# The gated merge, output projection and retrieval scores of a decoder layer in two halves of the tokens, and 160 gathered tokens in place of 128

## The chip, the core and the metric

The kernel runs on one core of one Trainium2 chip. The core has five engines with a program each: TensorE (PE) multiplies matrices, VectorE (DVE) and ScalarE (ACT) work element by element, GpSimd (POOL) here issues gathers, SyncE (SP) issues transfers. They meet through semaphores. Data comes from HBM by 16 DMA engines into SBUF, which has 128 partitions; PE writes to PSUM. The metric is the device time of one launch in microseconds, lower is better; the median of several runs counts.

## The reference

One layer of a decoder for 512 tokens of 2048 float32 features: two token mixers side by side (a gated linear recurrence, HGRN2, and a latent attention, MLA), a gated merge and an output projection, then the PEER mixer, a gated embedding and a last norm. What the change touches:

```python
y = sigmoid(ga) * (o_a @ w_a) + sigmoid(gb) * (o_b @ w_b)    # ga, gb: two products of the normed input
x = x + y @ w_o
x = x + peer_ffn(rms_norm(x, norm_ffn), peer_wq, peer_k1, peer_k2, peer_u, peer_v)
hp = rms_norm(x, norm_ple)
x = x + sigmoid(hp @ w_pg) * (p @ w_pe)
...
def peer_ffn(h, wq, k1, k2, u_tab, v_tab):      # 8 heads, 128 keys in each half, 16384 experts
    q = (h @ wq).reshape(N, HEADS, 2, 128)
    s1, s2 = q[:, :, 0] @ k1.T, q[:, :, 1] @ k2.T
    v1, i1 = top_k(s1, 16); v2, i2 = top_k(s2, 16)
    cand = (v1[..., :, None] + v2[..., None, :]).reshape(N, HEADS, 256)
    cv, ci = top_k(cand, 16)
    e = i1[ci // 16] * 128 + i2[ci % 16]         # 8 heads * 16 = 128 experts for a token
    gate = softmax(cv)
    z = einsum('thkd,td->thk', u_tab[e], h)
    return einsum('thk,thkd->td', gelu(z) * gate, v_tab[e])
```

## The kernel before

**Products.** Each float32 product is done as three float32r matmuls of a high and a low part (`mm3`, L147 to L149: high by high, low of the data by high of the weights, high of the data by low of the weights). Weights come in blocks of 128x2048 (1 MB), each in two halves: SP loads a half into one of four `raw` buffers, ACT makes the high part (`hi`, L111), DVE the low part (`lo`, L112), in rings of four. `Ahead` loads a block two steps before it is used and splits it one step before. A block holds 16 tiles of 128x128, so 48 matmuls, whose width is the number of tokens that pass through (512, or 384 in PEER's dense part).

**Stages.** The recurrence runs to about 460 us, then attention. The gates are 32 weight blocks put between the attention heads and beside the loading of the merge's inputs (`FILL`, `fill_in`). Then come merge (`w_a`, `w_b`), output projection (`w_o`, with the sum of squares for the next norm), the embedding (`w_pe`, 96 matmuls), each for all 512 tokens, and the normed input h of PEER in 16 chunks (`h_chunk`, L682). Up to here a scheduler orders the instructions by their dependencies; from the query product on the order is written by hand (`manual_schedule`).

**PEER.** The 512 tokens are treated in two ways. The first 128 (group A, `NA`) gather the rows of their experts: POOL issues an indirect DMA for one of 128 slots (a row of 2048 for each of 128 tokens, 1 MB), DVE multiplies it by h and sums (`dot_u`, L785), and in the second half adds it to the output with its coefficient (`axpy_v`, L1083). The other 384 (group B, `NB`) go through all 16384 experts densely: 128 blocks of U (L1028), whose result z goes through gelu to HBM (`z_s`); a matrix of gates is built from one-hot rows (`gate_tokens`, L833, L843) and stored (`G_s`); 128 blocks of V multiply the product of the two (L1003, split by L154 and L155, added up by L1091). The top-k of the scores, by repeated MAX, index and replace (L692 to L697), runs on DVE in steps with costs written by hand, spread over the query product (group A) and over U (three groups of 128 tokens in group B). In V one row is added per block, in 120 of 128 blocks. Two row buffers serve the gathers.

**Queues.** SP issues weight loads and the loads of z and gates; ACT issues the stores of z and of scores, and an issue that waits holds what is behind it on ACT; POOL issues the gathers.

Of the kernel before, what the change touches and what calls it, by code (L numbers as in the profile page):

```python
# [22 lines left out]
KT = 16  # L23
NA = 128
NB = T - NA
# [21 lines left out]
def kernel(ctx: ExitStack, tc: tile.TileContext, a, dbg=None):  # L47
# [14 lines left out]
    # ---------------------------------------------------------------- helpers  # L62
# [14 lines left out]
    class Ring:  # L77
        """Buffers taken in turn."""
# [42 lines left out]
    class Ahead:  # L121
        """Streams of a list of blocks: loaded two steps ahead, split one step ahead."""
# [28 lines left out]
    def split(hi, lo, src, gain=None):  # L151
        """hi + lo = src * gain, both float32r."""
# [7 lines left out]
    def cols_proj(src, xh, xl, kt=KT):  # L160
        """PSUM [128 output columns, T] for one column tile."""
# [6 lines left out]
    def rows_proj(srcs, blocks, before=None):  # L168
        """PSUM [128 tokens, 512 columns] for each token block."""
# [12 lines left out]
    def rstd_cols(ss, n, name):  # L182
        """[128 tokens, blocks] of 1/sqrt(ss/n + eps)."""
# [13 lines left out]
    def sums_over_features(sq):  # L197
        """[128 tokens, 4] PSUM sums over the partitions of sq [128, T]."""
        ps = mx()
        for b in range(4):  # L200
            TE.matmul(ps[:, b:b + 1], lhsT=sq[:, b * 128:(b + 1) * 128], rhs=ones[:, :1],
                      start=True, stop=True)
        return ps[:, :4]
# [14 lines left out]
    class SumSq:  # L218
        """Sum of squares of [128, T] chunks over features."""

        def __init__(self, acc=None):
            self.acc = tmp.tile([128, T], F32, name="sqacc", bufs=1) if acc is None else acc
            self.n = 0

        def add(self, x):
            if self.n == 0:
                S.activation(self.acc, x, AF.Square)
            else:
                s = t2()
# [8 lines left out]
    # ---------------------------------------------------------------- constants  # L238
    masks = const.tile([128, 384], F32R, name="masks")
# [3 lines left out]
    tril = const.tile([128, 128], U32, name="tril")  # L243
# [16 lines left out]
    # ---------------------------------------------------------------- DRAM scratch  # L260
    ga_s = [dram.tile([128, T], F32, name=f"ga{i}") for i in range(16)]
    gb_s = [dram.tile([128, T], F32, name=f"gb{i}") for i in range(16)]
# [4 lines left out]
    pe_s = [dram.tile([128, T], F32, name=f"pe{i}") for i in range(16)]  # L267
    z_s = dram.tile([128 // NJ, 128, NJ, NB], F32, name="z_s")
    G_s = dram.tile([NB // TC, 128, 128 * TC], F32, name="G_s")

    # ---------------------------------------------------------------- x * gain, split
# [11 lines left out]
    hg = tc.alloc_tile_pool(name="hg", bufs=1, side="left")  # L283

# [15 lines left out]
    # ---------------------------------------------------------------- HGRN2  # L300
# [172 lines left out]
    # rotary tables: angle = position * frequency, reduced to [-pi, pi]  # L473
# [36 lines left out]
    gates_todo = [(a["w_ga"][i], ga_s[i]) for i in range(16)] + [(a["w_gb"][i], gb_s[i]) for i in range(16)]  # L510
    FILL = (0, 2)
# [864 lines left out]
```

## Time and profile before

| what | value |
|---|---|
| runs | 4041.33, 4042.06, 4043.58 us, median 4042.06 |
| profiled execution, span from first to last instruction | 4040.0 us |
| PE busy | 4005.3 us (99%) |
| DVE, ACT, POOL busy | 2621.1, 1597.2, 347.6 us |
| mean granted PE clock | 0.998 |
| moved by DMA | 862.68 MB, 214 GB/s in the mean |

The page gives one execution, whose span of 4040.0 us is the profiled time itself; the runs were timed apart from it and lie 1.3 to 3.6 us above. PE is busy almost throughout, and a busy engine is the first candidate for what sets the time; whether the others merely keep up is read stage by stage, from the busy time in windows and from who waits for whom.

### The profile page before, as it was taken

The numbers are of one execution on the slowest core, as the hardware profiler recorded it, in microseconds if no ns is written. First come the engines' busy times: TensorE is split into PE (matmuls) and PEld (weight loads), VectorE is DVE, ScalarE is ACT, GpSimd is POOL, SyncE is SP. The second block draws the span as 40 slices with busy tenths as digits, with TensorE's granted clock in tenths as the row PEclk, the third lists the DMA queues.
The fourth block names the chain that finished last, engine by engine and source line by source line (L and its number), as shares of the span: only waits on it lengthen the run. The fifth ranks groups of instructions, "written<-read, shape, count | busy, mean of one in ns | idle before, by whom it ended". The sixth has DMA issues, their size and how long they took to land. (4 is left out here: it accounts for less than half of the span.)

```text
span 4040.0 us, 54629 instructions
## 1 busy us (share of the span) xinstructions
PE 4005.3 (99%) x21191; PEld 3667.2 (91%) x21191; DVE 2621.1 (65%) x3992; ACT 1597.2 (40%) x2582; POOL 347.6 (9%) x262
## 2 busy tenths in 40 slices
PE   9999999999999999999999999999999999999998
PEld 7878777778888889999999999999999999999976
DVE  5352554443343343699998998977777888877744
ACT  5342433332332242325566555753333333333443
POOL 0000000000000000021221211111111111111000
PEclk9999999999999999999999999999999999999999
DMA  5222222334444442478787788789888888888432
GB/s 210 97 74 94 72 96 84 102 105 141 151 141 133 141 140 99 166 286 304 283 303 283 287 302 298 293 332 356 317 297 315 312 311 312 299 313 310 169 117 97
DMA packets 264515, 862.68 MB, mean 214 GB/s; under 512 B 24128, under 2 KB 94272, under 8 KB 229568
## 3 DMA queue, kind: packets, MB, share of 16 engines
q1 hardware_dynamic: 202064, 531.57, 38.5%
q0 software_dynamic: 36864, 268.45, 17.8%
q10 hardware_dynamic: 25328, 59.17, 3.8%
q8 instruction: 168, 2.75, 0.3%
q14 instruction: 91, 0.75, 0.1%
HBM read 780.44 MB, written 78.64 MB: 213 GB/s over the span
## 5 line engine op out<-in xcount | busy, mean ns | idle before, releaser
L111 ACT ACTIVATE hi<-raw 128x1024 fp32r<-128x1024 f32 x806 | 851.4, 1059 | 1606.9 <-PE acc L148 1371.9
L112 DVE TENSOR_TENSOR lo<-raw,hi 128x1024 fp32r<-128x1024 f32 x806 | 975.0, 1221 | 782.6 <-ACT hi L111 779.5
L147 PE MATMUL acc<-hBh,hi 128*128 128x384 f32 x2304 | 775.0, 336 | 0.0
L148 PE MATMUL acc<-hBl,hi 128*128 128x384 f32 x2304 | 774.5, 336 | 0.0
L149 PE MATMUL acc<-hBh,lo 128*128 128x384 f32 x2304 | 774.4, 336 | 0.0
L148 PEld LDWEIGHTS acc<-hBl,hi 128*128 128x128 f32 x2304 | 433.1, 188 | 3.0 <-DVE hBl L155 0.2
L147 PEld LDWEIGHTS acc<-hBh,hi 128*128 128x128 f32 x2304 | 433.1, 188 | 2.7
L149 PEld LDWEIGHTS acc<-hBh,lo 128*128 128x128 f32 x2304 | 433.1, 188 | 0.0
L779 POOL DMA_INDIRECT row<-in_peer_u_dram,eA x128 | 198.9, 1554 | 2551.1 <-DMA raw<-in_uT_dram 1703.2
L149 PE MATMUL acc<-xh,lo 128*128 128x512 f32 x912 | 363.9, 399 | 0.0
L147 PE MATMUL acc<-xh,hi 128*128 128x512 f32 x912 | 363.4, 398 | 0.0
L148 PE MATMUL acc<-xl,hi 128*128 128x512 f32 x912 | 362.6, 398 | 0.0
L147 PE MATMUL acc<-ahx,hi 128*128 128x384 f32 x1024 | 344.7, 337 | 0.0
L148 PE MATMUL acc<-alx,hi 128*128 128x384 f32 x1024 | 344.1, 336 | 0.0
L149 PE MATMUL acc<-ahx,lo 128*128 128x384 f32 x1024 | 344.1, 336 | 0.0
L147 PE MATMUL acc<-ah,hi 128*128 128x384 f32 x1024 | 344.1, 336 | 0.0
L148 PE MATMUL acc<-al,hi 128*128 128x384 f32 x1024 | 344.1, 336 | 0.0
L149 PE MATMUL acc<-ah,lo 128*128 128x384 f32 x1024 | 344.1, 336 | 0.0
L1083 DVE SCALAR_TENSOR_TENSOR outA<-row,coef,outA 128x2048 f32<-128x2048 f32 x127 | 298.0, 2346 | 16.6 <-DMA row<-in_peer_v_dram,eA 16.3
L785 DVE SCALAR_TENSOR_TENSOR row<-row,hrow 128x2048 f32<-128x2048 f32 x128 | 292.0, 2283 | 20.5 <-DMA row<-in_peer_u_dram,eA 20.4
L779 POOL DMA_INDIRECT row<-in_peer_v_dram,eA x128 | 147.5, 1152 | 860.3 <-DVE outA L1083 799.6
L149 PEld LDWEIGHTS acc<-xh,lo 128*128 128x128 f32 x912 | 171.4, 188 | 43.0 <-issue 2.4
(379 smaller groups left out, 6270.5 us busy)
## 6 DMA issues: line engine op xcount, KB each, us to landing
raw<-in_uT_dram SPq DMA_DIRECT2D x256, 512.0 KB, 6.9
raw<-in_vB_dram SPq DMA_DIRECT2D x256, 512.0 KB, 5.7
z_s<-t ACTq DMA_DIRECT2D x128, 192.0 KB, 4.9
G_s<-stage ACTq DMA_DIRECT2D x12, 2048.0 KB, 14.4
zt<-z_s SPq DMA_DIRECT2D x32, 768.0 KB, 7.4
gt<-G_s SPq DMA_DIRECT2D x32, 768.0 KB, 12.1
raw<-in_w_ga_dram SPq DMA_DIRECT2D x32, 512.0 KB, 3.5
raw<-in_w_gb_dram SPq DMA_DIRECT2D x32, 512.0 KB, 3.5
```

Of the source, the lines that this page charges most:

```text
L111: S.activation(hi, raw, AF.Copy)
L112: V.tensor_tensor(lo, raw, hi.bitcast(F32), op=OP.subtract)
L147: TE.matmul(out, lhsT=lh, rhs=rh, start=start, stop=False)
L148: TE.matmul(out, lhsT=lh, rhs=rl, start=False, stop=False)
L149: TE.matmul(out, lhsT=ll, rhs=rh, start=False, stop=stop)
L779: G.indirect_dma_start(out=row, out_offset=None, in_=tab, in_offset=bass.IndirectOffsetOnAxis(ap=eA[:, s:s + 1], axis=0))
L785: V.scalar_tensor_tensor(row, row, 1.0, hrow, op0=OP.mult, op1=OP.mult, accum_out=zA[:, s:s + 1])
L1083: V.scalar_tensor_tensor(outA, row, coef[:, s:s + 1], outA, op0=OP.mult, op1=OP.add)
```

## The change

Tokens 0 to 255 (the first half) now go through gates, merge, output projection, embedding, norm and scores before tokens 256 to 511 (the second half) do the same; each half multiplies 256 columns, so the weights of gates, `w_a`, `w_b`, `w_o`, `w_pe` and `wq` are loaded and split twice. The first half is left to the scheduler; the second is part of the order written by hand. While it runs, `background` does the top-k of token groups 0 and 1 and the first 26 dots of gathered rows. The gathered tokens grow from 128 to 160: the 32 new ones (`NX`) are spread over 128 partitions as 4 slots for each token, so their 128 experts take 32 gathers in U and 32 in V. The dense part has 352 columns (`ND`). Gathers have three row buffers. The query product makes columns for all tokens, where before group A's part was made by rows and transposed.

The diff, cut to its core (comments and docstrings are removed throughout, too, and line numbers move):

```diff
 NA = 128
-NB = T - NA
+NX = 32
+RX = 128 // NX
+ND = T - NA - NX
+NE = H - NA - NX
...
-        ps = cols_proj(src, xh, xl)
-        t = t2()
-        V.tensor_tensor(t, ps, rr_mix, op=OP.mult)
+        w = Stream(src)
+        ps = acc()[:, :H]
+        for k in range(KT):
+            mm3(ps, *w.part(k, KT), xh[:, k, :H], xl[:, k, :H], k == 0, k == KT - 1)
+        t = t2()[:, :H]
+        V.tensor_tensor(t, ps, rr_mix[:, :H], op=OP.mult)
...
+    def block(src):
+        if not manual[0]:
+            return Stream(src)
+        w = ahead.step()
+        run_late()
+        background()
+        return w
+
...
+    def embed_half(hf, ph, pl, sq, rr):
+
+        for i in range(2):
+            w = block(a["w_pe"][i])
+            for m in range(0, 8, 2):
+                ps = mx()
+                for c in range(2):
+                    for k in range(2):
+                        mm3(ps[:, c * H:c * H + H], *w.part((m + c) * 2 + k, 16), ph[:, k], pl[:, k], k == 0, k == 1)
+                t = t2()
+                S.activation(t, ps, AF.Copy)
+                nc.scalar.dma_start(flat(pe_s[hf][i * 4 + m // 2]), t)
+                if (i, m) == (0, 2):
+                    rc = rstd_cols(sums_over_features(sq.acc), D, "rc_ffn")
+                if (i, m) == (1, 2):
+                    rows_of(rc, rr)
+            done()
+
+    def h_chunk(k, x1, rr, hh, hl, kept=None):
+        t = t2()[:, :H]
+        V.scalar_tensor_tensor(t, x1[:, k], g_ffn[:, k:k + 1], rr, op0=OP.mult, op1=OP.mult)
+        split(hh, hl, t)
+        if kept is not None:
+            nc.scalar.dma_start(kept, t[:, NA + NX:])
+
...
+                S.activation(q, ps, AF.Copy)
+                return lambda: keys(i, q)
+
+            if manual[0]:
+                late.append(lambda query=query, turn=turn: turn.append(query()))
+            else:
+                query()()
+        return turn
+
...
-    def h_chunk(kt):
-        t = t2()
-        V.scalar_tensor_tensor(t, x1[:, kt], g_ffn[:, kt:kt + 1], rr, op0=OP.mult, op1=OP.mult)
-        split(hAh[:, kt], hAl[:, kt], t[:, :NA])
-        split(hBh[:, kt], hBl[:, kt], t[:, NA:])
...
+    embed_half(0, ph, pl, sq, rr)
+    for k in range(KT):
+        h_chunk(k, x1, rr, hAh[:, k], hAl[:, k], hd_s[:, k])
...
+    for k in range(KT):
+        r = t2()[:, :H]
+        nc.sync.dma_start(r, a["xT"][k][:, H:])
+        V.scalar_tensor_tensor(r, r, g_mix[:, k:k + 1], rr_mix[:, H:], op0=OP.mult, op1=OP.mult)
+        split(xBh[:, k], xBl[:, k], r)
...
-            t["scores"] = upool.tile([128, 16, 128], F32, name="scores")
-            if b:
-                nc.sync.dma_start(flat(t["scores"]), sc_s[b])
-            else:
-                scores_A.append(t["scores"])
+            t["scores"] = kpool.tile([128, 16, 128], F32, name="scores")
+            nc.scalar.dma_start(flat(t["scores"]), sc_s[b])
...
-    pending = None
-    for cg in range(4):
-        qA, qB = mx(), [acc()[:, :NB] for _ in range(4)]
-        for kq in range(4):
-            if cg == 0:
-                for k in range(4):
-                    h_chunk(kq * 4 + k)
-            w = ahead.step()
...
+    NEARLY = 26
+    todo = prep_A() + merge(prep_B(1), [(2.5, dot_u)] * NEARLY)
+    NB2 = 80
+    todo = phase(NB2, todo)
+    spent, at = [0.0], [0]
+
+    def background():
+        at[0] += 1
+        hold[0] = max(0, hold[0] - 1)
+        while todo and spent[0] < at[0] and not hold[0] and len(after_pe) < 2:
+            c, f = todo.pop(0)
+            f()
+            spent[0] += c
+
...
+    for n, (src, dst) in enumerate((("w_ga", ga_s[1]), ("w_gb", gb_s[1]))):
+        for i in range(16):
+            w = block(a[src][i])
+            ps = acc()[:, :H]
+            for k in range(KT):
+                mm3(ps, *w.part(k, KT), xBh[:, k], xBl[:, k], k == 0, k == KT - 1)
+
+            def gate(i=i, ps=ps, dst=dst):
+                t = t2()[:, :H]
+                S.activation(t, ps, AF.Sigmoid)
+                nc.scalar.dma_start(dst[i], t)
+
+            late.append(gate)
+            after_products()
+            if n:
+                mixed(i, 1, oh, ol)
+    run_late()
...
+    embed_half(1, ph, pl, sq, rr)
+    for k in range(KT):
+        h_chunk(k, x1, rr, hBh[:, k, NE:], hBl[:, k, NE:])
+    last_keys = scores_half(1, lambda k: hBh[:, k, NE:], lambda k: hBl[:, k, NE:])
...
+    upool = tc.alloc_tile_pool(name="upool", bufs=1, side="left")
+    NF, NW = 3, 116
+    MIX = (36, 46)
+    prep = prep_B(2)
+    work = phase(MIX[0], merge(prep[:-1], quads[1]) + prep[-1:])
+    prep = prep_B(3)
+    work += phase(MIX[1], merge(prep[:-1], quads[2]) + prep[-1:])
+    work += phase(NW - NF - sum(MIX), quads[3])
...
-        z = acc()[:, :NB]
+            spent += c
+        while dots[0] and LEFT + 1 - dots[0] <= LEFT * n / (NU - 2) + 1e-9:
+            dot_u()
+        z = acc()[:, :ND]
...
-            late = []
+            run_late()
             act_mul(grp + 1, dp)
-            while axpys and 129 - len(axpys) <= 128 * (n + 1) / NV + 1e-9:
-                axpy_v(axpys.pop(0))
+            while axpys and NDOT + 1 - axpys <= NDOT * (n + 1) / NV + 1e-9:
+                axpys -= 1
```

Three places in the order of the instructions, as the programs stand. The first is ACT's program at the seam between the halves: `t` are chunks of the second half's input, `xBh` their high parts, `scores<-sc_187` the issue of the load of group 0's scores, `hi_78` the high part of a gate block's weights.

```order
L158 ACTIVATE xBh<-t_10336 128x256
L859 DMA scores<-sc_187 128x2048
L158 ACTIVATE xBh<-t_10341 128x256
L158 ACTIVATE xBh<-t_10346 128x256
L158 ACTIVATE xBh<-t_10351 128x256
L158 ACTIVATE xBh<-t_10356 128x256
L158 ACTIVATE xBh<-t_10361 128x256
L158 ACTIVATE xBh<-t_10366 128x256
L158 ACTIVATE xBh<-t_10371 128x256
L158 ACTIVATE xBh<-t_10376 128x256
L158 ACTIVATE xBh<-t_10381 128x256
L115 ACTIVATE hi_78<-raw_74 128x1024
```

The stores of the last scores (`sc_187`, `sc_188`) stand directly ahead of these rows; before, neither chunks of the input nor a score load stood between the gates and the merge. The second is DVE at the same seam; `xBl` are the chunks' low parts, `val` the largest scores of group 0.

```order
L159 TENSOR_TENSOR xBl<-t_10361,xBh 128x256
L819 SCALAR_TENSOR_TENSOR t_10366<-t_10366,gains,rr_mix 128x256
L846 MAX val<-scores 128x8 x2
L848 MAX_INDEX idx<-val,scores 128x8
L159 TENSOR_TENSOR xBl<-t_10366,xBh 128x256
L819 SCALAR_TENSOR_TENSOR t_10371<-t_10371,gains,rr_mix 128x256
L819 SCALAR_TENSOR_TENSOR t_10376<-t_10376,gains,rr_mix 128x256
L819 SCALAR_TENSOR_TENSOR t_10381<-t_10381,gains,rr_mix 128x256
L159 TENSOR_TENSOR xBl<-t_10371,xBh 128x256
L159 TENSOR_TENSOR xBl<-t_10376,xBh 128x256
L159 TENSOR_TENSOR xBl<-t_10381,xBh 128x256
```

Behind these rows come the other chunks, then eight additions `t<-hAh,hAl` for h by rows, and then the low parts of the next blocks. Before, group A's MAX stood behind parts of the query product. The third is DVE at the norm ahead of the query product: first of before, where `lo` are low parts of weights.

```order
L682 SCALAR_TENSOR_TENSOR t_9288<-x_8051,gains,rr_ffn 128x512
L155 TENSOR_TENSOR hAl<-t_9288,hAh 128x128
L155 TENSOR_TENSOR hBl<-t_9288,hBh 128x384
L682 SCALAR_TENSOR_TENSOR t_9294<-x_8051,gains,rr_ffn 128x512
L155 TENSOR_TENSOR hAl<-t_9294,hAh 128x128
L155 TENSOR_TENSOR hBl<-t_9294,hBh 128x384
L112 TENSOR_TENSOR lo_80<-raw_72,hi_76 128x1024
L112 TENSOR_TENSOR lo_81<-raw_73,hi_77 128x1024
L682 SCALAR_TENSOR_TENSOR t_9366<-x_8051,gains,rr_ffn 128x512
```

Four chunks stood there for each weight block. In the changed kernel, second half, a lookup and a dot stand ahead and the chunks stand in one piece, 16 of them, before the next weights:

```order
L116 TENSOR_TENSOR lo_82<-raw_74,hi_78 128x1024
L116 TENSOR_TENSOR lo_83<-raw_75,hi_79 128x1024
L929 SCALAR_TENSOR_TENSOR row_7019,zA<-row_7019,hrow 128x2048
L215 TENSOR_SCALAR t_14999<-cst,rc_ffn 128x128 x2
L723 SCALAR_TENSOR_TENSOR t_15037<-x_B,gains,rrB 128x256
L159 TENSOR_TENSOR hBl<-t_15037,hBh 128x256
L723 SCALAR_TENSOR_TENSOR t_15041<-x_B,gains,rrB 128x256
L159 TENSOR_TENSOR hBl<-t_15041,hBh 128x256
L723 SCALAR_TENSOR_TENSOR t_15045<-x_B,gains,rrB 128x256
```

The place of V, where the rows are added, reads as follows in the changed kernel (`hrow` is now the sum of the gathered rows, `x` the dense one, `zt` and `gt` the z and the gates that come back):

```order
L1231 TENSOR_TENSOR x_26682<-x_26682,acc 128x352
L1150 TENSOR_TENSOR zt_26266<-zt_26266,gt_26268 128x352
L1222 SCALAR_TENSOR_TENSOR hrow<-row_7017,zA,hrow 128x2048
L1222 SCALAR_TENSOR_TENSOR hrow<-row_7018,zA,hrow 128x2048
L159 TENSOR_TENSOR alx_26696<-zt_26266,ahx_26688 128x352
L1231 TENSOR_TENSOR x_26682<-x_26682,acc 128x352
L116 TENSOR_TENSOR lo_82<-raw_74,hi_78 128x1024
L116 TENSOR_TENSOR lo_83<-raw_75,hi_79 128x1024
L1231 TENSOR_TENSOR x_26682<-x_26682,acc 128x352
L1150 TENSOR_TENSOR zt_26266<-zt_26266,gt_26268 128x352
```

Every third block now has two rows, where before all but a few had one.

## Rows read from the trace of the kernel before

**Rows 1.** The page, its head and section 1: busy us, share, instructions by engine.

```profile
span 4040.0 us, 54629 instructions
...
PE 4005.3 (99%) x21191; PEld 3667.2 (91%) x21191; DVE 2621.1 (65%) x3992; ACT 1597.2 (40%) x2582; POOL 347.6 (9%) x262
```

**Rows 2.** Busy time by stage: embedding, scores, U, V.

```profile
core 0: us, PE busy (x) PEld busy (x) DVE busy (x) ACT busy (x) POOL busy (x), PEclk, DMA share, GB/s
...
1424.00:1446.00 22.00, 22.00 (x99) 17.60 (x98) 7.02 (x16) 13.32 (x21) 0.00 (x0) 1.00 0.71 239
1446.00:1650.00 204.00, 202.64 (x1146) 193.33 (x1145) 94.88 (x239) 67.03 (x106) 0.00 (x0) 1.00 0.31 104
1650.00:2771.00 1121.00, 1114.18 (x6522) 1108.81 (x6521) 988.97 (x1790) 610.91 (x1275) 203.02 (x130) 1.00 0.80 293
2771.00:3769.00 998.00, 998.00 (x5760) 998.00 (x5759) 794.73 (x847) 318.53 (x363) 143.40 (x126) 1.00 0.87 310
```

**Rows 3.** Busy time in stretches of one width, and in U; columns as above.

```profile
1260.00:1410.00 150.00, 150.00 (x645) 120.75 (x644) 49.88 (x53) 35.37 (x40) 0.00 (x0) 1.00 0.43 138
1700.00:2650.00 950.00, 943.18 (x5514) 937.81 (x5514) 861.68 (x1595) 537.00 (x1147) 182.16 (x115) 1.00 0.80 295
2900.00:3700.00 800.00, 800.00 (x4617) 800.00 (x4616) 638.76 (x680) 254.30 (x290) 116.47 (x102) 1.00 0.87 310
```

**Rows 4.** Timeline of PE, first and last of 12 matmuls of 256 columns.

```profile
564.03 0.28 PE L560 MATMUL acc<-hi,ch_kv 128*128 128x256 f32 x1
...
565.32 0.28 PE L562 MATMUL acc<-hi,cl_kv 128*128 128x256 f32 x1
```

**Rows 5.** Groups of DVE by line and shape: busy us, mean ns, idle before.

```profile
L1083 DVE SCALAR_TENSOR_TENSOR outA<-row,coef,outA 128x2048 f32<-128x2048 f32 x127 | 298.0, 2346 | 16.6 <-DMA row<-in_peer_v_dram,eA 16.3
L785 DVE SCALAR_TENSOR_TENSOR row<-row,hrow 128x2048 f32<-128x2048 f32 x128 | 292.0, 2283 | 20.5 <-DMA row<-in_peer_u_dram,eA 20.4
L833 DVE SCALAR_TENSOR_TENSOR ohr<-cst,slots 128x256 fp32r<-128x256 f32 x384 | 157.6, 477 | 0.1
...
L1228 DVE TENSOR_TENSOR x<-x,wide 128x256 f32<-128x256 f32 x32 | 10.9, 411 | 0.8 <-PE wide L212 0.8
```

**Rows 6.** Timeline of ACT, then DVE, at the norm ahead of the scores.

```profile
1450.29 0.31 ACT L154 ACTIVATE hAh<-t 128x128 fp32r<-128x128 f32 x1 [1.29 <-DVE t L682]
1450.51 0.51 ACT L154 ACTIVATE hBh<-t 128x384 fp32r<-128x384 f32 x1
...
1449.51 0.75 DVE L682 SCALAR_TENSOR_TENSOR t<-x,gains,rr_ffn 128x512 f32<-128x512 f32 x1
1450.63 0.29 DVE L155 TENSOR_TENSOR hAl<-t,hAh 128x128 fp32r<-128x128 f32 x1 [0.38 <-ACT hAh L154]
...
1456.02 2.36 DVE L112 TENSOR_TENSOR lo<-raw,hi 128x1024 fp32r<-128x1024 f32 x2 [0.39 <-ACT hi L111]
```

**Rows 7.** Score stores: issue on ACT, landing; then the landing of score loads.

```profile
L907 ACTq DMA_DIRECT2D sc<-t x12: 326/326/349, 1518.6 to 1662.7; - x12
...
DMA to landing us min/median/max: 2.3/2.8/14.2
...
DMA to landing us min/median/max: 7.3/10.9/14.2
```

**Rows 8.** DMA queues from 2900 to 3700 us: packets, MB, share of 16 engines.

```profile
q1 hardware_dynamic: 68425, 138.70, 49.2%
q0 software_dynamic: 14872, 108.28, 37.3%
```

**Rows 9.** Busy time in short stretches; columns as in rows 2.

```profile
3525.00:3550.00 25.00, 25.00 (x146) 25.00 (x145) 21.43 (x22) 8.00 (x10) 3.04 (x3) 1.00 1.02 387
...
4020.00:4030.00 10.00, 3.43 (x18) 2.52 (x18) 8.89 (x31) 2.89 (x5) 0.00 (x0) 0.76 0.45 150
```

**Rows 10.** Waits of DVE in V, then of PE in U: us, times, longest.

```profile
DVE outA L1083 <- DMA row<-in_peer_v_dram,eA: 16.3, 7, 4.4
...
PE wide L843 <- DVE ohr L833: 5.1, 4, 1.8
```

More of the change, by code (lines that the diff above doesn't have):

```diff
@@ L602, with after, run_late @@
     ml.release()
-    opool = tc.alloc_tile_pool(name="opool", bufs=1, side="left")
-    oh = opool.tile([128, 16, T], F32R, name="oh")
-    ol = opool.tile([128, 16, T], F32R, name="ol")
+    late = []
+    manual = [False]
+    def after(f):
+        if manual[0]:
+            late.append(f)
+        else:
+            f()
+    def run_late():
+        todo = late[:]
+        late.clear()
+        for f in todo:
+            f()
+    def block(src):
[5 more added lines that the diff above has]
+        return w
@@ new lines, in residual_half, with res @@
+    def residual_half(hf, yh, yl, x1, sq):
+        s = slice(hf * H, hf * H + H)
+        for mt in range(16):
+            r = t2()[:, :H]
+            nc.sync.dma_start(r, a["xT"][mt][:, s])
+            w = block(a["w_o"][mt])
+            ps = acc()[:, :H]
+            for k in range(KT):
+                mm3(ps, *w.part(k, KT), yh[:, k], yl[:, k], k == 0, k == KT - 1)
+            def res(mt=mt, ps=ps, r=r):
+                V.tensor_tensor(x1[:, mt], ps, r, op=OP.add)
+                sq.add(x1[:, mt])
+                nc.scalar.dma_start(x1_s[mt][:, s], x1[:, mt])
+            after(res)
+            done()
@@ new lines, in h_chunk, with scores_half, keys, evac @@
+    def h_chunk(k, x1, rr, hh, hl, kept=None):
[4 more added lines that the diff above has]
+            nc.scalar.dma_start(kept, t[:, NA + NX:])
+    def scores_half(hf, hh, hl):
+        sc = [None, None]
+        def keys(i, q):
+            for b in range(2):
+                if i % 4 == 0:
+                    sc[b] = mx()
+                TE.matmul(sc[b][:, i % 4 * 128:i % 4 * 128 + 128], lhsT=q[:, b * 128:b * 128 + 128],
+                          rhs=kk_t[:, i % 2], start=True, stop=True)
+            if i % 4 == 3:
+                def evac(sc=sc[:]):
+                    for b in range(2):
+                        t = t2()
+                        S.activation(t, sc[b], AF.Copy)
+                        nc.scalar.dma_start(sc_s[hf * 2 + b][:, (i // 4) * 512:(i // 4) * 512 + 512], t)
+                after(evac)
+        turn = []
+        for i in range(16):
+            w = block(a["wq"][i])
+            ps = acc()[:, :H]
+            for k in range(KT):
+                mm3(ps, *w.part(k, KT), hh(k), hl(k), k == 0, k == KT - 1)
+            for f in turn:
+                f()
+            turn = []
+            done()
+            def query(i=i, ps=ps):
+                q = t2()[:, :H]
+                S.activation(q, ps, AF.Copy)
+                return lambda: keys(i, q)
+            if manual[0]:
+                late.append(lambda query=query, turn=turn: turn.append(query()))
+            else:
+                query()()
+        return turn
@@ new lines @@
+    p_half(1, ph, pl)
+    sq = SumSq(n=H)
+    residual_half(1, yh, yl, x1, sq)
+    ypool.release()
+    hpool = tc.alloc_tile_pool(name="hpool", bufs=1, side="left")
+    hBh = hpool.tile([128, KT, ND], F32R, name="hBh")
+    hBl = hpool.tile([128, KT, ND], F32R, name="hBl")
+    for c in range(4):
+        t = t2()[:, :4 * NE].rearrange("p (k t) -> p k t", k=4)
+        s = slice(c * 4, c * 4 + 4)
+        nc.sync.dma_start(t, hd_s[:, s])
+        split(hBh[:, s, :NE], hBl[:, s, :NE], t)
+    embed_half(1, ph, pl, sq, rr)
@@ L977 @@
     spent = 0.0
[L978 to L980 removed]
     def finish(z, j):
[L983 removed]
+        zg = t2()[:, :ND]
         S.activation(zg, z, AF.Gelu)
@@ L1097, in v_products @@
         return ps
-    late = []
-    axpys = list(range(128))
+    axpys = NDOT
     NV = (NGRP - 1) * 8
@@ L1150 @@
         cur = ahead.step()
-        for f in late:
-            f()
-        late = []
+        run_late()
         ps = [v_products(cur, NGRP - 1, half) for half in range(2)]
@@ L1187 @@
         pe = t2()
-        nc.sync.dma_start(pe, pe_s[mt])
+        for h in range(2):
+            nc.sync.dma_start(pe[:, h * H:h * H + H], pe_s[h][mt // 2][:, mt % 2])
         cur = ahead.step()
-        for f in late:
-            f()
-        late = later
+        run_late()
+        late += later
         later = []
@@ L1266 @@
     tl.release()
+    hr.release()
     psW.release()
```

494 lines of the change are left out of this document (236 added, 258 removed).

## The prediction

> **What bounds the kernel now.** I read the page first: in a span of 4040.0 us TensorE (PE) is busy 4005.3 us [rows 1]. Then busy time by stage [rows 2]: in the embedding and the V half PE is busy in the whole stretch at full clock; the U half leaves 6.8 us idle (1121 − 1114.18), the score stage 1.4. So time is won only by taking away PE columns, and lost only where something new makes PE wait. VectorE (DVE), which the change loads further, is already busy 988.97 of 1121 us in U and 794.73 of 998 in V. Third, the spacing of matmuls by width: 645 in 150 us with 512 columns, 232.6 ns each; 4617 in 800 us with 384, 173.3 ns [rows 3]; 256 columns start 11 steps apart in 1.29 us, 117.3 ns [rows 4]. Price per column hardly changes, 0.454, 0.451, 0.458 ns, and a weight load before each stays hidden.
>
> **The change part by part.**
>
> 1. Halves instead of whole rows (gates, merge, output projection, embedding, queries). Programs counted: 3361 matmuls of 512 columns and 768 of 384 (a part of the query product) go, 919.6 us with 233.5 ns as the step of a single 512; 7842 of 256 come, 917.5 us with 117. The balance is −2.
>
> 2. Dense half at 352 columns. 12288 matmuls shrink by 32 columns. On the line from 256 to 384 (56.0 ns per 128 columns) one saves 14.0 ns, on the line from 384 to 512 (59.3 to 60.2) 14.8 to 15.1, in proportion 14.4. That is 172 to 185 us; I take **−175**. The page "TensorE: Matmul & The Clock Gate" of the Trainium skill, section Back-to-back issue gap, gives N/2.4 + 2.5 ns for a single matmul; by it 384 would stand at 162.5 (the trace: 173.3), and 32 columns would be worth 13.3 ns, an estimated 164 us. The rows are nearer to this kernel, and the sum goes by them.
>
> 3. Weights twice. 82 blocks are loaded and split again. A 256-column block gives PE 48 × 0.117 = 5.63 us. Its two low parts cost DVE 2.36 us, read from the pair [rows 6]; ScalarE (ACT) is loaded less. Both fit where nothing else is due. In the second half's merge DVE also has, per block, some eight 128x256 operations over two blocks (0.41 each, [rows 5]: 1.66) and the background's share, the top-k of two groups (about 54 us each after overlap, a third of what U's three groups cost) and 26 dots of 2.28, so about 170 us over 80 blocks, 2.1. The sum is 5.6 to 5.9 of 5.63: DVE-bound or just not, 0 to 20 us over 16 blocks; I take **+6**. Elsewhere in that half it is about 5.0 and PE covers it: nothing. If the cover went, 50 blocks by 0.3 us would cost 15, which lies in the range.
>
> 4. The norm of the first half. Before, 96 matmuls of 512 columns in the embedding (22 us) cover the chain from the sum of squares to the first h chunk, and four chunks were made per weight block of 16 us. Now the cover is 96 × 0.117 = 11.2 us and all 16 chunks stand ahead of the queries. Per chunk DVE has a scaled copy of 128x256 (0.477 less overlap, 0.40) and a low part (0.33), ACT a high part (0.40, between 0.31 for 128 columns and 0.51 for 384, [rows 6]) and a DMA issue of 0.326 [rows 7]: 11.7 us on either engine, one dependent chunk about 1.05, of which PE's first block covers 5.6. Bounds 8 and 13; I take **+10**.
>
> 5. The seam between the halves. The first gate block of the second half needs 16 xB chunks, made behind the last query block: 16 × 0.73 = 11.7 us on DVE, then eight additions for h by rows, 8 × 0.61 = 4.9. In their midst on DVE stands the first MAX of group A's scores, which waits for a load; such a load landed 7.3 to 14.2 us after issue [rows 7]. On ACT its issue stands between high parts and itself waits for the last score store, which lands in 2.3 us at the least. Whoever is queued behind is late: low parts, then PE's gate block. Without these waits 12, with them 22; I take **+16**.
>
> 6. The norm of the second half. Here the order is written by hand: scaled copy, high, low, one chunk after another. The trace has the three legs of such a chain: the copy starts at 1449.51, the high part at 1450.29, the low part at 1450.63 and ends at 1450.92 [rows 6]. A width of 256 gives 1.27 us a chunk (0.45, 0.40, 0.35 and hand-overs), 20.3 for 16, and DVE does the next step only after it. A dot of 2.28 and lookups stand ahead of the chain. PE has one block, 5.6 us, to spread over it. 20.3 − 5.6 = 14.7 at the least; with the dot and two lookups of some 0.7 each 18, and if PE, idle so long, comes back at a lower clock (granted 0.76 in the stretch 4020 to 4030, where it was busy 3.43 us [rows 9]) up to 28. I take **+22**.
>
> 7. U. Three groups' top-k become two and the gate matrix loses 32 tokens: of DVE's 7.9 us a block (861.68 us in 950, [rows 3]) some 0.8 go, 7.1 of the new 7.98. That is 90% as before, and the 6.8 us of idle time, of which 5.1 stood behind the one-hot rows [rows 10], should shrink: **−5** (bounds −7 and +10).
>
> 8. V. A block takes PE 8.32 us now and would take 7.63. DVE: 638.76 us over 96 blocks, 6.64; narrower tiles −0.18, a third more gathered rows +0.26 × 2.346 = +0.61: 7.07, 92% of a block against 80%. The waits behind are small: DVE stood 16.3 us on rows in all [rows 10], and the third row buffer keeps the lead of a row (two blocks of 7.63 less one addition, 12.9 us) near that of before (two of 8.32 less one, 14.3). The queues are another matter. In 800 us of V the two main ones moved 138.70 and 108.28 MB at 49.2% and 37.3% of the engines [rows 8]; the first is 1.443 MB a block. Afterwards a block needs 1.41 MB and 1.333 × 1.048 = 1.40 MB in 7.63 us; at the bytes per share of these rows that is 52.5% + 50.5% = 1.03 of the engines, 368 GB/s, and in the first eight blocks 4.2 MB of the residual besides. The best stretches of V show 1.02 and 387 GB/s [rows 9]. The 120 blocks hold 341 MB: at 387 they are hidden (881 us against 916), at the share's price they take 943. Bounds 0 and +60; I take the share's price, **+27**. By the page "DMA: Bandwidth & Descriptors" of the Trainium skill, section Specifications, the limit of HBM for one core is some 358 GB/s, which would make an estimated 953 us, +37; the trace has stretches above it.
>
> 9. A third gate is filled in per attention head, and the V end has transposes and sums for the 32 tokens (eight blocks, two more transposes and four small additions each, taken like the 0.41 of [rows 5] at most): **+3**.
>
> The sum against the profiled execution: 4040.0 − 2 − 175 + 6 + 10 + 16 + 22 − 5 + 27 + 3 = 3942 us. The median of the runs, 4042.06, lies 2.1 above that execution's span, so **3944**.
>
> **Rivals.**
> - *All covered.* The scheduler lets gate blocks of the first half or the embedding run under the chunks, and the queues hold 387 GB/s: of the +79 only some 15 stay. 4042 − 177 + 15, so 3870 to 3900. For it: PE lost 1.4 us in the whole score stage before. Against it: the order below shows the chunks in one piece.
> - *V is bound by its queues.* At 350 GB/s, between the mean of now and the best stretch, 341 MB last 974 us, 31 more than summed; with the waits that a late row hands to the low parts behind it on DVE, 60: 3975 to 4005. For it: 92% DVE, share 1.03. Against it: 387 GB/s for 25 us with PE undisturbed [rows 9].
> - *Slower than before.* The mechanism is the same place, deeper: two queues at the limit, DVE in program order, so a row that is late holds the low parts, then PE. It decides once V lasts 106 us longer than summed, 1049 us or 8.74 a block; that is a rate under 325 GB/s. For it: 310 were moved at a share of 0.87 [rows 3], which leaves the limit near 356. Against it: the stretch of [rows 9] with a share of 1.02 moved 387. Time 4055 to 4090.
> - *352 columns cost what 384 did.* Then −175 falls away: some 4119. The three spacings lie on one line, so hardly.
>
> **How the numbers follow.** Forecast 0.57 (its own range 3910 to 3970); all covered 0.16; V bound by its queues 0.19; slower 0.05; no narrower matmul 0.02; 0.01 in between. The range reaches into the first two rivals, 3890 to 4000; outside lie half of the first, a sixth of the second and the slow cases, 0.18. 0.2% is 8 us, about what a measurement of this kernel can tell from no change. Faster by more: all but the slow cases and a thin strip, 0.92; within 0.02; slower 0.06.
>
> **What the new profile would show.** Matmuls of 352 columns near 159 ns and of 256 near 117 (steps 1, 2). A U block near 8.0 us and a V block near 7.85 rather than 7.63, with DMA shares about 1.0 (8). Gaps of PE: 10 us before the first query block, 16 at the seam with DVE's MAX waiting for scores, over 15 before the second query stage behind the chunk chain (4 to 6). I am wrong if V runs undisturbed (then about 3917), if gaps lie inside the second half's weight blocks (cover of step 3 gone), or if PE's clock drops for longer than the gaps.

## The result and the profile after

The changed kernel takes 4065.09 us in the median (4059.98 to 4065.97, four runs) against 4042.82 for the kernel before on the same chip: a ratio of 1.0051, 95% interval [1.0037, 1.0065]. The forecast was 3944, 3890 to 4000. The profiled execution has a span of 4064.2 us.

The page of the changed kernel, head and section 1 [rows 1 before]:

```profile
span 4064.2 us, 63784 instructions
...
PE 3948.1 (97%) x24921; PEld 3742.2 (92%) x24921; DVE 2946.7 (73%) x4421; ACT 1744.0 (43%) x2800; POOL 528.8 (13%) x326
```

PE works 57 us less than before (4005.3), and yet the span is 24 longer: idle time rose from 35 to 116 us. Its mean granted clock fell from 0.998 to 0.986. Where, the windows by stage say: first half's merge, output projection, embedding, queries; then the second half's gates, merge, projection, embedding, queries; U; V; its last group; the end. Columns as in [rows 2].

```profile
890.00:985.00 95.00, 93.28 (x766) 92.28 (x766) 64.69 (x102) 53.34 (x88) 0.00 (x0) 0.98 0.75 238
985.00:1076.00 91.00, 91.00 (x775) 91.00 (x774) 52.62 (x68) 39.41 (x50) 0.00 (x0) 1.00 0.75 231
1076.00:1091.00 15.00, 12.69 (x105) 12.34 (x103) 6.44 (x15) 10.79 (x17) 0.00 (x0) 1.00 0.67 226
1091.00:1198.00 107.00, 103.63 (x828) 99.75 (x828) 51.32 (x64) 47.42 (x70) 0.00 (x0) 0.97 0.62 190
1198.00:1440.00 242.00, 203.78 (x1573) 196.32 (x1572) 160.44 (x387) 91.40 (x136) 5.76 (x6) 0.93 0.63 206
1440.00:1548.00 108.00, 93.55 (x768) 91.91 (x768) 93.80 (x221) 41.63 (x53) 11.76 (x7) 0.98 0.80 269
1548.00:1641.00 93.00, 92.75 (x769) 92.58 (x770) 81.70 (x146) 39.83 (x51) 10.07 (x6) 0.98 0.86 290
1641.00:1672.00 31.00, 17.41 (x105) 16.60 (x103) 16.37 (x28) 13.49 (x22) 1.87 (x2) 0.78 0.77 271
1672.00:1788.00 116.00, 113.74 (x830) 106.53 (x830) 81.55 (x105) 51.24 (x78) 13.52 (x8) 0.90 0.67 232
1788.00:2841.00 1053.00, 1050.31 (x6509) 1047.12 (x6509) 906.62 (x1445) 579.97 (x1196) 225.73 (x134) 1.00 0.86 311
2841.00:3796.00 955.00, 943.11 (x5761) 938.98 (x5760) 845.37 (x878) 305.32 (x364) 258.88 (x157) 1.00 0.94 354
```

A half's merge, projection or queries are 768 matmuls of 117 ns, 90 us; the 32 gate blocks are 1536, 180 us; the embedding is 96, 11 us. Against that the second half's gates took 242, its merge 108, its embedding and queries 31 + 116; the first half's merge 95, embedding and queries 15 + 107. U's first product (in the trace of before the 769th of the 6912 with `hBh` and `hBl`, the first 768 being queries) starts at 1640.9 us there and at 1788.1 here: 147 us more up to there, where the forecast had 55. U takes 1053 (before 1130; forecast 1037), V's 120 blocks 955 (before 998; forecast 943). The rest is 3 us shorter.

The waits of PE between 1198 and 1440 us, that is, in the second half's gates (us, times, longest):

```profile
PE acc L153 <- DVE lo L116: 12.4, 12, 4.3
PE acc L151 <- ACT hi L115: 9.0, 10, 2.6
PE acc L151 <- ACT xBh L158: 7.6, 4, 3.9
PE acc L152 <- DVE xBl L159: 6.3, 3, 5.7
```

They are waits for both parts of the weights and for the chunks, in a stage in which DVE is busy 160 of 242 us: no engine is full. ACT's program there shows why (timeline of 11 us, two gate blocks; in brackets the idle time ahead and what ended it):

```profile
1336.47 0.42 ACT L158 ACTIVATE ohB<-t 128x256 fp32r<-128x256 f32 x1 [4.53 <-DMA t<-oa]
1336.80 1.99 ACT L115 ACTIVATE hi<-raw 128x1024 fp32r<-128x1024 f32 x2
1338.69 0.36 ACT L1080 ACTIVATE t<-acc 128x256 f32<-128x256 f32 x1
1339.08 0.34 ACTq L1081 DMA_DIRECT2D gb<-t  x1
1339.46 0.45 ACTq L646 DMA_DIRECT2D t<-oa  x1
1343.95 0.42 ACT L158 ACTIVATE ohB<-t 128x256 fp32r<-128x256 f32 x1 [4.89 <-DMA t<-oa]
1344.27 1.99 ACT L115 ACTIVATE hi<-raw 128x1024 fp32r<-128x1024 f32 x2
1346.16 0.36 ACT L1080 ACTIVATE t<-acc 128x256 f32<-128x256 f32 x1
```

ACT issues the load of a mixer's output (`t<-oa`), and the next instruction in its program needs it: it stands 4.9 us for the landing, and the high parts of the weights stand behind it. One turn takes 7.5 us, a block of PE 5.63. `mixed` loads a tile of that output and splits it (into its high and low part) in one go. In the first half the scheduler had put other work between the two: ACT waits there at most 3.9 us for such a load, and PE 0.2 us in all from 460 to 890 us. The order written by hand keeps the two together.

### The profile page after: what moved, and what is told of

Same layout as the page of the kernel before. It is cut to its first block, busy times and chain, and to the rows that moved or that the text cites. A ratio compares the mean times of both kernels' runs of the same rounds, so it can differ in the third digit from the quotient of the medians.

```text
span 4064.2 us, 63784 instructions
## 1 busy us (share of the span) xinstructions
PE 3948.1 (97%) x24921; PEld 3742.2 (92%) x24921; DVE 2946.7 (73%) x4421; ACT 1744.0 (43%) x2800; POOL 528.8 (13%) x326
## 5 line engine op out<-in xcount | busy, mean ns | idle before, releaser
L116 DVE TENSOR_TENSOR lo<-raw,hi 128x1024 fp32r<-128x1024 f32 x970 | 1168.6, 1221 | 671.0 <-ACT hi L115 666.1
L151 PE MATMUL acc<-hBh,hi 128*128 128x352 f32 (+1 forms) x2304 | 746.8, 324 | 3.1 <-ACT hBh L158 2.5
L153 PE MATMUL acc<-hBh,lo 128*128 128x352 f32 (+1 forms) x2304 | 742.1, 322 | 0.5 <-DVE lo L116 0.5
L152 PE MATMUL acc<-hBl,hi 128*128 128x352 f32 (+1 forms) x2304 | 739.2, 321 | 0.2
L151 PE MATMUL acc<-ahx,hi 128*128 128x352 f32 x1024 | 335.3, 327 | 4.1 <-DVE x L1231 4.1
L153 PE MATMUL acc<-ahx,lo 128*128 128x352 f32 x1024 | 333.9, 326 | 1.9 <-DVE lo L116 1.9
L151 PE MATMUL acc<-ah,hi 128*128 128x352 f32 x1024 | 334.7, 327 | 0.1
L152 PE MATMUL acc<-al,hi 128*128 128x352 f32 x1024 | 330.9, 323 | 3.4 <-DVE al L159 3.4
L153 PE MATMUL acc<-ah,lo 128*128 128x352 f32 x1024 | 333.5, 326 | 0.7 <-DVE lo L116 0.7
L152 PE MATMUL acc<-alx,hi 128*128 128x352 f32 x1024 | 331.0, 323 | 1.7 <-DVE alx L159 1.7
L151 PE MATMUL acc<-xh,hi 128*128 128x256 f32 (+1 forms) x912 | 305.0, 334 | 0.0
```

What stands on the lines that cost most here:

```text
L116: V.tensor_tensor(lo, raw, hi.bitcast(F32), op=OP.subtract)
L151: TE.matmul(out, lhsT=lh, rhs=rh, start=start, stop=False)
L152: TE.matmul(out, lhsT=lh, rhs=rl, start=False, stop=False)
L153: TE.matmul(out, lhsT=ll, rhs=rh, start=False, stop=stop)
```

## The experiments

**The load ahead of its split.** The load for block i is issued while block i − 1 runs:

```diff
+            g = n * 16 + i - 15
+            if 0 <= g < 16:
+                nxt = t2()[:, :H]
+                nc.scalar.dma_start(nxt, (oa_s + ob_s)[g][:, H:])
             if n:
-                mixed(i, 1, oh, ol)
+                split(oh[:, i], ol[:, i], r_in)
+            if 0 <= g < 16:
+                r_in = nxt
```

> The changed kernel with one edit: in the second half's 16 blocks of the second gate, the load of a mixer's output is issued one block before it is split, so that ACT no longer stands behind a load that it has only just issued. Theory A (that wait, 4.5 us of an ACT chain of 7.3 us in blocks of 5.63, is what PE stood for between 1325 and 1440 us): the stretch falls by 25 to 35 us with the clock it cost, the kernel to about 4035. Rival B (the weight loads or DVE's background are late there, and the wait only fills slack): within 8 us of 4065.

Measured: 4029.84 us, ratio to before 0.9975 [0.9964, 0.9987]; 35 us less than the changed kernel, as theory A had it; 33 of them lie between the last query product and the first product of the second merge (244.1 to 211.5). In this run's windows the same blocks keep PE busy at full clock:

```profile
1325.00:1350.00 25.00, 25.00 (x214) 25.00 (x213) 21.76 (x32) 12.74 (x18) 0.00 (x0) 1.00 0.74 242
1350.00:1375.00 25.00, 25.00 (x214) 25.00 (x213) 18.47 (x28) 14.39 (x20) 2.01 (x2) 1.00 0.72 230
1375.00:1400.00 25.00, 20.10 (x159) 19.90 (x159) 15.96 (x30) 7.03 (x12) 2.81 (x3) 0.93 0.98 388
```

What is left at 1375 to 1400 is another wait of that kind: the first dot of a gathered row stands in DVE's program too soon behind its gather, and PE waits 4.9 us for the low parts behind it. DVE's row of it, in this run and then in the changed kernel:

```profile
1381.46 2.29 DVE L929 SCALAR_TENSOR_TENSOR row<-row,hrow 128x2048 f32<-128x2048 f32 x1 [9.91 <-DMA row<-in_peer_u_dram,eA]
...
1403.50 2.29 DVE L929 SCALAR_TENSOR_TENSOR row<-row,hrow 128x2048 f32<-128x2048 f32 x1 [8.51 <-DMA row<-in_peer_u_dram,eA]
```

**The seam.** Chunks loaded ahead into row buffers, and the score load on POOL's queue:

```diff
+    for k in range(KT):
+        nc.sync.dma_start(xs[k], a["xT"][k][:, H:])
     scores_half(0, lambda k: hAh[:, k], lambda k: hAl[:, k])
...
-        nc.sync.dma_start(r, a["xT"][k][:, H:])
-        V.scalar_tensor_tensor(r, r, g_mix[:, k:k + 1], rr_mix[:, H:], op0=OP.mult, op1=OP.mult)
+        V.scalar_tensor_tensor(r, xs[k], g_mix[:, k:k + 1], rr_mix[:, H:], op0=OP.mult, op1=OP.mult)
...
-            nc.scalar.dma_start(flat(t["scores"]), sc_s[b])
+            nc.gpsimd.dma_start(flat(t["scores"]), sc_s[b])
```

> The changed kernel with two edits at the seam: the 16 chunks of the second half's input are loaded ahead into row buffers that are still free, and the score load is issued on POOL's queue. Theory A (PE's idle time at 1197 to 1217 us comes from DVE's wait of 7.1 us on a chunk's load and ACT's of 4.8 us on the score store): 10 to 16 us less, about 4053. Rival B (the chunks' own work on DVE, 11.7 us, and eight additions bound the seam anyway): 0 to 4 us less.

Measured: 4058.5 us, 1.0044 [1.0027, 1.0061], 6.6 less, between the two theories, and the intervals of this run and of the changed kernel overlap. From the last query product to the first product of the second merge it took 232.5 us instead of 244.1; some 5 of these 12 went again ahead of it, where the first half's merge and queries were slower beside the earlier loads (from the merge's first product to the last query product 313.0 instead of 307.6). The two waits were there in the changed kernel (timelines at the seam, DVE's two rows and then ACT's, which waits for the score store):

```profile
1204.25 0.48 DVE L819 SCALAR_TENSOR_TENSOR t<-t,gains,rr_mix 128x256 f32<-128x256 f32 x1 [0.59 <-DMA t<-in_xT_dram]
1211.80 0.49 DVE L819 SCALAR_TENSOR_TENSOR t<-t,gains,rr_mix 128x256 f32<-128x256 f32 x1 [7.06 <-DMA t<-in_xT_dram]
...
1207.57 1.03 ACT L158 ACTIVATE xBh<-t 128x256 fp32r<-128x256 f32 x3 [4.76 <-DMA sc<-t]
```

Around them PE did 57 matmuls in 25 us, and its clock fell (windows of the changed kernel):

```profile
1200.00:1225.00 25.00, 11.00 (x57) 9.13 (x56) 14.49 (x40) 8.87 (x20) 0.00 (x0) 0.66 0.57 176
```

So the waits were real and about half of the seam; what stays is the chunks' own work, which in the run without the waits holds DVE from 1207 to 1221 us.

**The second half's norm.** The kept columns (h of the first half's dense tokens, stored and loaded again) are split beside the query blocks, the last residual is added first, and DVE scales two chunks ahead:

```diff
-    for c in range(4):
...
-        split(hBh[:, s, :NE], hBl[:, s, :NE], t)
-    embed_half(1, ph, pl, sq, rr)
-    for k in range(KT):
-        h_chunk(k, x1, rr, hBh[:, k, NE:], hBl[:, k, NE:])
+    run_late()
+    embed_half(1, ph, pl, sq, rr, (0, 6), (1, 4))
+    for k in range(KT + 2):
+        if k < KT:
...
+            S.activation(hBh[:, k, NE:], t, AF.Copy)
...
+        if k >= 2:
...
+            V.tensor_tensor(hBl[:, j, NE:], scaled_h[j], hBh[:, j, NE:].bitcast(F32), op=OP.subtract)
```

> The changed kernel with edits at the second half's norm only: the kept h columns are loaded and split beside the query blocks, the last residual is added before the embedding, the sums and the row of the norm are taken later among the embedding's products, and DVE scales two chunks ahead of the low part. Theory A (the hand-written chain, 16 chunks at 1.30 us, and PE's waits of 7.8 and 4.3 us for the sums, with the low clock after them): 20 to 30 us less, about 4040. Rival B (PE would wait for weights or the chain of the norm all the same): less than 8 us.

Measured: 4045.94 us, 1.0013 [1.0004, 1.0023]; 19 less, just under what theory A had. PE's wait for the sum of squares fell from 7.8 to 0.6 us; the one for the row of the norm stayed (5.7 us). In the changed kernel the chain of chunks on DVE stood as forecast, 1.30 us from one to the next:

```profile
1672.09 0.48 DVE L723 SCALAR_TENSOR_TENSOR t<-x_B,gains,rrB 128x256 f32<-128x256 f32 x1
1673.05 0.43 DVE L159 TENSOR_TENSOR hBl<-t,hBh 128x256 fp32r<-128x256 f32 x1 [0.48 <-ACT hBh L158]
1673.39 0.48 DVE L723 SCALAR_TENSOR_TENSOR t<-x_B,gains,rrB 128x256 f32<-128x256 f32 x1
```

and ahead of it PE had waited for the sum of squares, which was behind a dot, the kept columns and a weight block on DVE; it came back at half its clock (timeline of PE):

```profile
1651.74 1.01 PE L206 MATMUL mx<-ones,sqacc 128*128 128x1 f32 x4 [7.78 <-DVE sqacc L236]
...
1653.40 0.41 PE L151 MATMUL mx<-phB,hi 128*128 128x256 f32 x1
1653.62 0.41 PE L152 MATMUL mx<-plB,hi 128*128 128x256 f32 x1
```

**352 columns by themselves.** The kernel before with U and V cut to 352 columns, and then to 320; the last tokens get no expert part:

```diff
-        z = acc()[:, :NB]
+        z = acc()[:, :W]
         for k in range(KT):
-            mm3(z, *cur.part(k, KT), hBh[:, k], hBl[:, k], k == 0, k == KT - 1)
+            mm3(z, *cur.part(k, KT), hBh[:, k, :W], hBl[:, k, :W], k == 0, k == KT - 1)
```

> The kernel before with the dense part of U and V cut to 352 of its 384 columns (the last 32 tokens get no expert part), nothing else. Theory A (a width of 352 costs more than its share, by itself): matmuls 162 ns apart, as in the changed kernel. Rival B (162 is the price of the denser DVE, DMA or gathers in the changed kernel): 159 ns. Time 3890 to 3910 by A, 3865 by B, if DVE does not bind in U.

> The kernel before with the dense part of U and V cut to 320 of its 384 columns (the last 64 tokens get no expert part). The run with 352 had matmuls 162.1 ns apart in V. Theory A (a width off a multiple of 64 costs extra, 320 doesn't): 144 to 146 ns. Rival B (whatever lies between 256 and 384 costs some 3 ns more than the line): 148 to 149. U is then bound by DVE and V by neither; so the step is read in V.

Measured: 3936.48 and 3836.63 us, one execution each. The step is read in V, where PE is busy throughout (windows of the two runs):

```profile
3200.00:3400.00 200.00, 200.00 (x1235) 200.00 (x1234) 168.47 (x184) 66.64 (x78) 29.14 (x27) 1.00 0.90 324
```

```profile
3200.00:3300.00 100.00, 100.00 (x684) 100.00 (x683) 90.26 (x101) 34.77 (x42) 17.56 (x16) 1.00 0.96 355
```

352 columns: 200 us / 1235 = 161.9 ns; 320: 100 / 684 = 146.2. The line from 256 to 384 gives 159.3 and 145.3. So the 162 ns of the changed kernel (800 / 4934 = 162.1 where PE is busy throughout, in its run without additions below) belong to the width and not to the denser traffic (theory A of the first run); 320 columns lie 0.9 ns above the line, just above what its theory A had, and nearer to it than to B. That a multiple of 64 is what matters rests on one width each and stays open. The time of the first run, 3936, is above what theory A had: U, where DVE was 90% busy at 384 columns, got only 37 us shorter: PE waited 22 us there for DVE.

**V: gathers or additions.** The changed kernel without every fourth gather, and without every fourth addition:

```diff
-            G.indirect_dma_start(out=row, out_offset=None, in_=tab,
-                                 in_offset=bass.IndirectOffsetOnAxis(ap=e[:, s:s + 1], axis=0))
+            if not (len(order) < 160 and len(order) % 4 == 3):
+                G.indirect_dma_start(out=row, out_offset=None, in_=tab,
+                                     in_offset=bass.IndirectOffsetOnAxis(ap=e[:, s:s + 1], axis=0))
...
-        else:
+        elif s % 4 != 3:
             V.scalar_tensor_tensor(o, row, c[:, s:s + 1], o, op0=OP.mult, op1=OP.add)
```

> The changed kernel without every fourth gather of V (40 of 160; the addition is made all the same, on an older row, so the output of the gathered tokens is not the layer's). V's 120 blocks took 955 us in the changed kernel, where 48 matmuls of 162.1 ns a block would take 934. Theory A (the queues are the limit there): below 940. Rival B (DVE is): 950 or more.

> The changed kernel with all gathers of V, but without every fourth addition of a row (40 of 160, left out of the output). Theory A (the queues limit V): 950 or more for V's 120 blocks. Rival B (DVE, at 92% of a block, limits it): below 940.

Measured: 4049.21 and 4045.59 us, one execution each; V's 120 blocks 936 and 934 instead of 955. Each theory named one limit and either cure works, so each was wrong in one of the runs. The windows from 2900 to 3700 us of the changed kernel, of the run without gathers and of the run without additions:

```profile
2900.00:3700.00 800.00, 788.11 (x4807) 783.98 (x4806) 711.08 (x737) 253.71 (x302) 219.41 (x133) 1.00 0.94 356
```

```profile
2900.00:3700.00 800.00, 799.36 (x4924) 798.77 (x4923) 730.84 (x758) 263.32 (x310) 192.68 (x103) 1.00 0.87 320
```

```profile
2900.00:3700.00 800.00, 800.00 (x4934) 800.00 (x4933) 652.79 (x721) 268.33 (x309) 147.23 (x137) 1.00 0.97 365
```

Without the additions the queues moved 365 GB/s at a share of 0.97 and PE was busy throughout: they were not full at 356. What holds is in the waits of DVE in the same stretch of the changed kernel:

```profile
DVE zt L1150 <- DMA gt<-G_s: 43.9, 11, 6.0
DVE lo L116 <- ACT hi L115: 41.7, 34, 2.8
```

The load of the gates (`gt`) is late eleven times, up to 6.0 us; before it was late once, 0.2 us. DVE, 711 of 800 us busy and in program order, cannot make that up, and the additions into the accumulator, by which PE gets its buffers back, and the low parts are late in turn.

**Gates two blocks earlier.**

```diff
-            if dp % NQ == 0:
-                act_load(grp + 1, dp // NQ)
+            for m in ([0] if n == 0 else []) + [n + 2]:
+                if m % NQ == 0 and m < NV:
+                    act_load(m // 8 + 1, m % 8 // NQ)
```

> The changed kernel with one edit: in V the loads of z and gates are issued two blocks earlier. In the runs without a fourth of the gathers or of the additions V fell from 955 to 936 and 934 us alike, so neither alone is the limit. Theory A (a gate load that comes late holds DVE, which at 92% of a block cannot make it up; 43.9 us of such waits stood in 800 us): V's 120 blocks fall to 936 to 942, the kernel by 12 to 19 us. Rival B (the queues are full there, and whatever is issued earlier makes something else late, the rows or the weights): V stays within 5 us of 955.

Measured: 4047.05 us, 1.001 [1.0001, 1.0019]; 18 less, and V 938, where the runs that leave V as it is have 949 to 956. Theory A holds: the wait for `gt` is gone from DVE's list of the same stretch, where besides 1.4 us of another kind this is left:

```profile
DVE lo L116 <- ACT hi L115: 66.3, 64, 3.2
```

**The early dots.** None of the 26 dots in the second half:

```diff
-    NEARLY = 26
+    NEARLY = 0
```

> The changed kernel with none of the 26 dots in the second half; all 160 are in U. The second half's merge took 109.6 us from the last gate product to the first of the output projection, where 768 matmuls of 117 ns take 90. Theory A (DVE is over a block's 5.63 us there, as the sum of 5.6 to 5.9 had it): the merge falls to 95 to 100 us, while U, where DVE goes from 7.1 to 7.6 of a block's 7.8 us, rises by 5 to 20; the kernel stays within 10 us. Rival B (the merge's loss is the weights' landing or the wait at its end): the merge stays above 106 us.

Measured: 4049.26 us, 1.002 [1.0009, 1.0031]; 16 less, more than the 10 of theory A. From the last gate product to the first of the output projection it took 102.8 us instead of 109.9, between the two theories, and U rose by 6. Most of the gain lies ahead: the gate blocks took 220 us instead of 235. The wait of 8.5 us for the first gathered row is gone there, and three dots of 2.3 us with it; the two were not taken apart. So taking out the dots gave back some 7 of the 20 us that the changed kernel lost in the merge. DVE's work there, 93.8 us, is over PE's 90 but does not fill the 108. PE waited 8.1 us for DVE to release accumulators (L669), in six places, and 3.4 at the end for `phB`, whose load SP issued 5.5 us before ACT split it, so that ACT stood 5.1 us. The other 8 or so were not taken apart. In the second version below, with the background halved, the same measure gives 97.0 us; that version changes other things too, but it suggests that DVE's load counts for more than the dots.

**Everything together.** Two versions. The first has the load ahead, the norm, and the seam in a stronger form: the chunks and h by rows are made between the first half's query blocks; group 1's scores are loaded before they are searched, the first dot is later, and the background does half as much in the merge. The second adds the earlier gates in V and leaves the blocks before the norm without background. The core of both:

```diff
+        if 4 <= i < 12:
+            for k in (i * 2 - 8, i * 2 - 7):
...
+                split(xBh[:, k], xBl[:, k], r)
+        if 12 <= i < 16:
+            rows_of_h(hrow, 0, NA, [i - 12])
+            rows_of_h(hrowX, NA, NX, [i - 12])
...
-    todo = prep_A() + merge(prep_B(1), [(2.5, dot_u)] * NEARLY)
+    todo, todoB = prep_A(), prep_B(1)
+    todo.insert(11, todoB.pop(0))
+    todo += todoB[:4] + merge(todoB[4:], [(2.5, dot_u)] * NEARLY)
...
+    SHARE = [0] * 2 + [1.15] * 30 + [0.6] * 16 + [1.25] * 14 + [0] * 4 + [1.35] * 16
...
-        at[0] += 1
+        at[0] += SHARE[nth[0]]
```

> The changed kernel with the edits of the first three runs together, and more: the second half's chunks and h by rows are made between the first half's query blocks, group 1's scores are loaded a few blocks before they are searched and the first dot stands some blocks behind its gather, and the background does half as much in a merge block. Theory A (the lost time is waits at the places found, so that it adds up): 35 + 19 + 10 to 16 for the edits singly, 5 to 15 for the rest: 3980 to 3995, faster than before. Rival B (DVE at 90% of each block gives part of it back elsewhere): 4005 to 4025.

> The version of 3989 us with the same edit in V, and no background work in the last two blocks of the output projection and the two of the embedding of the second half, with the sums of the norm taken one step earlier. Theory A: 12 to 19 us less from V and 5 to 12 from the norm, 3960 to 3972. Rival B (V's queues): 3977 to 3985.

Measured: 3989.23 us, 0.9869 [0.9852, 0.9885], and 3968.4 us, 0.9817 [0.9803, 0.983]. Both as theory A had it. The first is 76 us below the changed kernel, where 35, 19 and 7 had been measured singly and the rest of its edits were not; the second takes off another 21, where the earlier gates alone had given 18. The windows of the second: the gates, the merge, embedding with queries, and V.

```profile
1207.00:1391.00 184.00, 182.24 (x1536) 181.62 (x1535) 146.62 (x380) 85.99 (x118) 7.80 (x7) 1.00 0.75 249
1391.00:1484.00 93.00, 90.77 (x769) 89.73 (x768) 79.20 (x175) 38.97 (x48) 8.39 (x5) 1.00 0.84 286
1587.00:1712.00 125.00, 115.82 (x928) 113.11 (x928) 98.14 (x134) 64.44 (x99) 16.72 (x11) 0.96 0.81 296
2764.00:3698.00 934.00, 933.76 (x5757) 933.47 (x5756) 849.35 (x879) 310.59 (x364) 253.37 (x157) 1.00 0.96 362
```

The gates take 184 us where 180 are PE's work, V 934 where 5760 × 161.9 ns are 933; about 15 us still go at the norm of this half. PE's mean granted clock is 0.994.

## Why the prediction was wrong

By the spans of the profiled executions the forecast said 98 us less, and 24 more came: 122 to explain.

1. *Halves (step 1)* held in the widths: 256 columns are 118 ns apart in the median, 512 are 233. But the sum mixed a step of 233.5 ns with 117; with the steps of its own rows, 232.6, 173.3 and 117.3, it gives +5 and not −2.
2. *352 columns (step 2)* was mis-sized. The sum took the line between 256 and 384; the width itself costs 161.9 ns, so 12288 matmuls save 140 us and not 175. That is **35** of the 122. The formula of the Trainium skill weighed there ("TensorE: Matmul & The Clock Gate", section Back-to-back issue gap) came nearer with its 164 us, though it puts 352 columns at an estimated 149.2 ns.
3. *Weights twice (step 3)* is the step that failed: "Both fit where nothing else is due" and "PE covers it: nothing". It added up how long DVE and ACT work in a block, which fitted, and did not ask what stands in their programs ahead of the splits: a load waited for by the instruction behind its issue, in 16 blocks. Taking it away gave back **35**, 2 us a block, where the step had priced the loss of its cover at 0.3. The first gathered row, waited for 8.5 us in the same way, and the merge, 18 over its 90 where 6 were set down (of 0 to 20), make some **20** more. In the merge the step's terms, 2.36, 1.66 and 2.1, add up to 6.1 a block and not to 5.6 to 5.9; DVE was busy 5.9 of it. The forecast's last sentence had named gaps inside these blocks as what would make it wrong.
4. *Norm of the first half (step 4)* took 4 us in the embedding and, above 97 for its queries and keys, 10 in the queries: 14 against 10. Merge and projection of that half took 6 more than their 180, which was not forecast; the waits that PE shows there (1.5 us) don't explain it, a clock of 0.98 does in part. It stays open.
5. *Seam (step 5)*: from the last query product at 1197.8 to 1225 us PE had some 7 us of work, so about 20 against 16. ACT's wait for the score store was as described. DVE's was another one: the MAX, which the step had waiting for its scores, did not wait, and DVE stood 7.06 us for a chunk of the second half's input, whose load SP issued at 1207.16 us, after 6.1 us of waiting for a score store; ACT's score load was issued at that same moment. Removing both waits gave 12 at the place and 6.6 in all.
6. *Norm of the second half (step 6)* was right in its mechanism, 1.30 us a chunk where 1.27 was forecast, and mis-sized: 147 us for embedding and queries against 108 of work, 39 and not 22. The 17 more are PE's waits for the sums (7.8 us) and for the row of the norm (4.3), ahead of the chain, and the half clock behind them.
7. *U (step 7)* held: it is 77 us shorter, 70 of them by the width (6144 matmuls by 11.4 ns), and the other 7 stand against −5. Its idle time fell from 6.8 to 2.7 us.
8. *V (step 8)*: +21 against +27, the size nearly right by luck, since the mechanism is another. Not the bytes bind: the late load of the gates in front of a DVE with no time left does, and two blocks of lead remove it.

35 + 35 + 20 + 17, less 2 in U and 6 in V, is 99. Small ones make the rest: 10 in the first half (merge, projection, norm), 4 at the seam, 3 in the second projection, 7 in the sum of step 1.

Of the rivals none had the cause: the time fell into the 4055 to 4090 of "slower", but that rival put its price in V, where it was not. The largest loss and several of the smaller ones are one thing: a hand-written order in which a load or a gather is waited for by an instruction right behind it. With these waits taken out, the norm's chain overlapped and the background spread anew, the changed kernel is 1.8% faster than the kernel before.

## What to carry to other kernels

A block's budget is kept by the longest in-order turn of an engine, waits for its own DMAs included; adding up busy times only says that a turn could fit. When work moves from a scheduler's order into one written by hand, look for every load whose user stands right behind it, on that engine and on those that wait for it, and give it a block of lead. In V an engine busy 89% of the time turned late transfers of a few us into stalls of PE. A price between two measured widths is measured rather than interpolated where 12,000 matmuls depend on it.

## What the runs showed of the hardware

In this kernel's products the step of a matmul does not lie on a line in the number of its columns: 117.3 ns at 256, 146.2 at 320, 161.9 at 352, 173.3 at 384, 232.6 at 512. And idle time of PE cost more than itself: after waits of 7.8 us for the sums and a slow chain of chunks its granted clock stood at 0.78 in the embedding and 0.90 in the queries of the second half, where 256 columns were up to 0.22 us apart, the lower of its two levels (1.2 GHz), instead of 0.117.
